# A decoder step on one core: how the kernel picks a free buffer, by the engine that used it last

## The chip, the cores and the metric

The kernel runs on one core of a Trainium2 chip. The metric is the device time of one execution in microseconds (us), the median of several runs. The core has a matrix engine (TensorE, PE in the profile, its weight loads PEld), three engines for element-wise work (VectorE or DVE, ScalarE or ACT, GpSimd or POOL), and SyncE (SP), which only starts transfers here. GpSimd starts transfers too: loads leave from SP's queue, intermediate stores from POOL's.

## The reference

One inference step of a small hybrid decoder, 1024 prompt tokens and 8 single-token samples, 2048 channels, in fp32. Layer 1 projects to a branch and a gate, pools the branch over trailing windows of 2, 4, 8 and 16 tokens, mixes groups of 512 channels, multiplies by silu(gate) and projects back. Layer 2 does sliding-window attention (128 tokens, 32 heads over 4 shared key/value heads, with sinks) on keys and values made from layer 1's output. Each layer ends in a layer norm.

```python
z = x @ w_in                                  # layer 1
u, gate = z[..., :D_POOL], z[..., D_POOL:]
d, new_state = multiscale_pool(u, prefix, pos)
d = jnp.einsum('btgc,gce->btge', d.reshape(...), w_grp).reshape(B, T, D_POOL) * scale
x = layer_norm(ALPHA * x + (d * jax.nn.silu(gate)) @ w_out, g_ln, b_ln)
k, v = shared_kv(x, pos, w_kv)
z = x @ w_in_b                                # layer 2
q, gate = rope_partial(z[..., :D_ATTN], pos), z[..., D_ATTN:]
o = attn_core(q, k, v, q_pos, k_pos, sinks)
x = layer_norm(ALPHA * x + (o * jax.nn.silu(gate)) @ w_out_b, g_ln, b_ln)
```

## The kernel before

**Tiles and phases.** The tokens are split into two chunks of 512 and 520 (512 prompt tokens and the 8 samples). Activations lie with channels on the 128 partitions and tokens along the free dimension. Ten phases run one after another (PHASES): `ai` (input projection, pooling and group mix of layer 1), `ao` (its output projection and norm), `bi` (keys, values, queries, gates and attention of layer 2), `bo` (output projection and norm), each for chunk 0 and chunk 1. Most phases multiply with Strassen's scheme: seven products of half width for a block of two by two (`seven`, L655 to L657), two start with plain products (`unit`, L683 to L685).

**fp32 by two parts.** Each weight tile and each activation tile is split in a high part, cast by ScalarE (L476 for weights, L766 for activations), and a low part, which VectorE subtracts (L491 and L775). Each product is three matmuls: high by high, high by low, low by high. One "unit" of a Strassen phase is 24 matmuls of 128x128 by 256 or 260 columns on one weight tile.

**The pipeline.** `begin` runs ahead of each unit e: it issues weight loads up to unit e+7 (`load_to`, L275), casts up to e+4 and subtractions up to e+3 (`cast_to`, `prep_to`). The loaded tile is read by the cast and by the subtraction and is then free; the two parts are free after the unit's matmuls. Results leave PSUM by ScalarE (L594, L600, L603, L609, L615, L628) and VectorE (L616, L621). Beside them run sums of weights for the scheme, made on the fly and stored for the other chunk (L281, L334, L424 to L430), sums of activations (`t_ops`, L823 to L827), pooling (`pool_tile`, L1031 to L1042, split at L263 and L264), the norms (`ln_gen`, `phase_out`, L1234, L1277 to L1289), and attention (rope L1621 and L1729; scores L1759; maxima L1776 to L1788; exponentials L1795; sums L1803; scaling L1808; transposes L1812, copied out at L1821 and L1822; values L1836; gating L1845, stored at L1848). `t_gen` and `sum_gen` are spread between the units as side work.

**What sets the order.** PE, DVE and ACT run in the order of the source: `in_order` ties each instruction to the one before it on its engine. SP and POOL are ordered by the framework's own scheduler. The framework puts a semaphore wait wherever a buffer or a value needs it, also between two instructions of one engine.

**The buffers.** All of this shares one pool, `Mem`: 53 slots of 128 x 1040 fp32, which can be given out whole (`full`) or by halves (`half`). Slots are given and released in the order of the source, long before the engines get there; a slot that is given again makes its first writer wait until the engines have really finished with it. Before the change, `release` stamps a half with a count of releases, plus 10 if it was the source of a store, and `full` and `half` take the slot with the smallest stamp, whoever asks and whoever used it last.

Of the kernel before, what the change touches and what calls it, by code (L numbers as in the profile page):

```python
# [95 lines left out]
class Slot:  # L96
# [14 lines left out]

    def free(self, stored=False):
        self.mem.release(self, 10 if stored else 0)


class View:
# [11 lines left out]

    def free(self):
        for s in self.slots:  # L130
            self.left[s] -= 1
            if not self.left[s]:
                s.free()


class Mem:


    def __init__(self, pool, n):
        self.pool = pool  # L140
        self.t = [None] * n
        self.f = [[0, 0] for _ in range(n)]
        self.clock = self.n = 0
# [39 lines left out]
class Kern:  # L183
# [88 lines left out]
    def load1(self, s, k, src):  # L272
        def go():
            s[k] = self.mem.full()
            self.nc.sync.dma_start(s[k].a[:, :1024], src)  # L275

        return go
# [124 lines left out]
    def sum_gen(self, name):  # L402
# [6 lines left out]
        held = {}  # L409

        def load(n):
            if n < len(parts) and n not in held:
                q, cs = parts[n]
                s = held[n] = self.mem.full()
# [71 lines left out]
    def prep_to(self, n):  # L486
        self.cast_to(n)
        while self.prepped < min(n, len(self.stream)):
            s = self.stream[self.prepped]
            hi, lo = self.hl[self.prepped], self.mem.full()  # L490
            self.nc.vector.tensor_sub(lo.r[:, :1024], s.src().a[:, :1024], hi.a[:, :1024])  # L491
# [75 lines left out]
    def seven(self, c, z0, z1, after, c11=None, split=False, own=None):  # L567
# [65 lines left out]
        def run(idx):  # L633
# [24 lines left out]
            for s in w:  # L658
                s.free()
            for g in range(2):  # L660
# [8 lines left out]
    def unit(self, done):  # L669
# [3 lines left out]
        for par in range(2):  # L673
            w = self.begin()
            wh, wl = (s.r for s in w)
            for k in range(8):
# [11 lines left out]
                if k == 7:  # L688
                    for a in w:
                        a.free()  # L690
                    if par == 1:
                        self.posts.append(lambda: done(ps))
# [47 lines left out]
    def x_load(self):  # L740
# [3 lines left out]
        TH = T // 2  # L744
        s = self.mem.full()
        if self.xseven:
# [63 lines left out]
    def x_used(self, k):  # L810
        if self.last:
            ss = self.X.pop(k)
            if not (self.shared and not self.strassen and k[0] == 1):
                for s in ss:
                    s.free()

    def t_ops(self, E, O, dst, kp, TH):

        nc = self.nc
        s = self.mem.full()  # L820
        t = s.v(4, TH)
# [8 lines left out]
    def t_gen(self, key):  # L830
# [3 lines left out]
        def load(kp):  # L834
            s[kp] = self.mem.full()
            self.nc.sync.dma_start(s[kp].v(2, T), self.act[key][:, 2 * kp : 2 * kp + 2, :])
# [13 lines left out]
    def j_steps(self, T, a, b, box, *free):  # L850

        def add():
            box["u"] = self.mem.half()
            self.nc.vector.tensor_add(box["u"].a[:, :T], a, b)
            for f in free:
                f.free()
# [12 lines left out]
    def j_sum(self, T, box, out):  # L869
# [3 lines left out]
        for s in [slice(0, T)] if T <= 512 else [slice(0, T // 2), slice(T // 2, T)]:  # L873
# [7 lines left out]
            out(s, ps)  # L881
        hl.free()

# [25 lines left out]
    def ln_gen(self, c, pre, acc, gc, bc, out, td):  # L909
# [9 lines left out]
        def load(p):  # L919
            if p < 8 and p not in pre:  # L920
                pre[p] = self.mem.full()
                nc.sync.dma_start(self.pair_view(pre[p], T), away(p))
# [22 lines left out]
        else:  # L945
            self.j_sum32(T, [a2[:, 0], a2[:, 1]], put)
            acc.free()
        yield
        w = self.mem.full()
        q, v = w.a[:, :T], w.a[:, TMAX : TMAX + T]  # L950
# [61 lines left out]
    def pool_tile(self, c, m, Us, ext, dd):  # L1012
# [11 lines left out]
        if ext is not None:  # L1024
            nc.scalar.copy(ext[:, i, :, 15], U[:, NST + TP : NST + T])
        bufs = [self.mem.full() for _ in range(2 if w > 2 else 1)]
        src, step, n = U, 1, 0
# [36 lines left out]
    def group_half(self, c, g, h, dd, sg):  # L1064
# [24 lines left out]
        for s in w:  # L1089
            s.free()  # L1090
        if h == 1:
            for k in range(4):
                dd[k][2].free()

        def post():
            G = self.mem.full()
            t = self.pair_view(G, T)
# [108 lines left out]
    def phase_out(self, c, res, nxt, last=None):  # L1206
# [8 lines left out]
        def x_in(p):  # L1215
            if p < 8:
                xs[p] = self.mem.full()
                nc.sync.dma_start(self.pair_view(xs[p], T), res[:, 2 * p : 2 * p + 2, :])
# [86 lines left out]
    def phase_end(self, c, xs, x_in, pre, acc, gc, bc, out):  # L1305
# [77 lines left out]
        def back(p):  # L1383
            pre[p] = self.mem.full()
            nc.sync.dma_start(tv(p), self.act["p", c][:, 2 * p : 2 * p + 2, :])
# [222 lines left out]
    def partner(self, s, n, T):  # L1608

        t = self.mem.full()  # L1610
        for a in range(4):
# [131 lines left out]
    def attend(self, c, t, at, s1, s2, late=False, ticks=CLOSE):  # L1743
# [8 lines left out]
        def score():  # L1752
# [10 lines left out]
            if lastq:  # L1763
                s.free()

# [44 lines left out]
        def turn():  # L1810
            for i in range(8):
                nc.tensor.transpose(  # L1812
                    PT[:, i * P : (i + 1) * P], x["sc"][:, i * P : (i + 1) * P], cst[:, K_ID : K_ID + P]
                )
            x["s"].free()

        def keep():


            x["w"], x["wp"] = self.mem.full(), self.mem.full()  # L1820
            nc.scalar.copy(x["w"].a[:, :1024], PT)  # L1821
# [6 lines left out]
        def values():  # L1828
            o = x["o"] = self.S[:, 1, :512] if late else self.psO()
            for b in range(NB):  # L1830
                bs = slice(b * P, (b + 1) * P)
                for n, (V, p) in enumerate(((self.V[b + 1], x["w"].a), (self.Vd[b], x["wp"].a))):
                    for j in range(2):
# [4 lines left out]
                        )  # L1838
            x["w"].free()
            x["wp"].free()  # L1840

        def gate():
            a = self.ao[c, t] = self.mem.half()
            z, j = self.sg.pop((c, t))
# [42 lines left out]
    def dec_keys(self, pr):  # L1887
        nc, io = self.nc, self.io
        s = self.dks = self.mem.full()
        dk = s.a[:, :1024].rearrange("p (b k) -> p b k", b=NDEC)  # L1890
# [8 lines left out]
    def decode(self, c, pr):  # L1899
# [7 lines left out]
        def v0():  # L1907
            x["v"] = self.mem.full()
            dv = x["dv"] = x["v"].a[:, :1024].rearrange("p (b k) -> p b k", b=NDEC)
# [421 lines left out]
```

## Time and profile before

| | |
|---|---|
| median of 3 runs | 2347.38 us (2345.62 to 2347.71) |
| the profiled execution | 2344.57 us |
| its span, first to last instruction | 2342.8 us |
| TensorE busy, share of the span | 98% |
| VectorE, ScalarE, GpSimd busy | 82%, 58%, 9% |
| granted TensorE clock, mean | 0.997 |
| transferred | 669.39 MB, mean 286 GB/s |

The times of the lines below are in us from the start of the span. "L491" is line 491 of the kernel; "m<-m,m" says which buffers are written and read (m is the pool, pD, pO, pS are PSUM, names like swob are DRAM). "[1.02 <-DVE m L491]" is the idle time ahead of an instruction and what ended it. In a list of waits, the three numbers are us in total, how often, and the longest. Some per cent of matmul records may be missing in a trace.

### The profile page before, as it was taken

The numbers are of one execution on the slowest core, as the hardware profiler recorded it, in microseconds if no ns is written. First come the engines' busy times: TensorE is split into PE (matmuls) and PEld (weight loads), VectorE is DVE, ScalarE is ACT, GpSimd is POOL, SyncE is SP. The second block draws the span as 40 slices with busy tenths as digits, with TensorE's granted clock in tenths as the row PEclk, the third lists the DMA queues.
The fourth block names the chain that finished last, engine by engine and source line by source line (L and its number), as shares of the span: only waits on it lengthen the run. The fifth ranks groups of instructions, "written<-read, shape, count | busy, mean of one in ns | idle before, by whom it ended". The sixth has DMA issues, their size and how long they took to land. (4 is left out here: it accounts for less than half of the span.)

```text
span 2342.8 us, 49652 instructions
## 1 busy us (share of the span) xinstructions
PE 2302.7 (98%) x19960; PEld 2202.7 (94%) x19960; DVE 1923.7 (82%) x2386; ACT 1365.4 (58%) x2502; POOL 202.3 (9%) x379
## 2 busy tenths in 40 slices
PE   8999999999999999999999999999999999999997
PEld 6899999999999999998777899999999999999997
DVE  8788988777878878868998898897777778889887
ACT  4454446544546557655464666685666668556656
POOL 0111110010000000000111111100000000000000
PEclk9999999999999999999999999999999999999999
DMA  8668789989889989999799766788776768699785
GB/s 293 213 242 310 272 287 343 328 290 326 299 302 328 323 286 329 320 339 325 262 330 360 254 235 225 253 297 279 249 249 231 231 199 299 230 355 371 268 303 196
DMA packets 252072, 669.39 MB, mean 286 GB/s; under 512 B 25760, under 2 KB 106560, under 8 KB 251840
## 3 DMA queue, kind: packets, MB, share of 16 engines
q1 hardware_dynamic: 206368, 501.14, 63.3%
q0 software_dynamic: 45472, 165.07, 18.2%
q8 instruction: 156, 2.56, 0.4%
q14 instruction: 76, 0.62, 0.1%
HBM read 471.01 MB, written 185.59 MB: 280 GB/s over the span
## 5 line engine op out<-in xcount | busy, mean ns | idle before, releaser
L655 PE MATMUL pD<-m,m 128*128 128x260 f32 (+1 forms) x4752 | 1346.2, 283 | 4.7 <-ACT pD L594 2.8
L657 PE MATMUL pD<-m,m 128*128 128x260 f32 (+1 forms) x4752 | 1340.3, 282 | 6.2 <-DVE m L491 6.1
L656 PE MATMUL pD<-m,m 128*128 128x260 f32 (+1 forms) x4752 | 1339.8, 282 | 1.1 <-DVE m L775 1.1
L491 DVE TENSOR_TENSOR m<-m,m 128x1024 fp32r<-128x1024 f32 x674 | 814.2, 1219 | 114.8 <-ACT m L476 59.7
L655 PEld LDWEIGHTS pD<-m,m 128*128 128x128 f32 x4752 | 895.5, 188 | 13.2 <-issue 5.1
L657 PEld LDWEIGHTS pD<-m,m 128*128 128x128 f32 x4752 | 895.9, 189 | 8.5 <-DVE m L491 8.5
L656 PEld LDWEIGHTS pD<-m,m 128*128 128x128 f32 x4752 | 895.5, 188 | 1.8 <-DVE m L775 1.3
L476 ACT CAST m<-m 128x1024 fp32r<-128x1024 f32 x674 | 703.4, 1049 | 251.5 <-DVE m L334 69.6
L683 PE MATMUL pD<-m,m 128*128 128x512 f32 x448 | 179.5, 401 | 8.1 <-ACT m L766 8.1
L684 PE MATMUL pD<-m,m 128*128 128x512 f32 x448 | 177.2, 395 | 1.0 <-DVE m L775 1.0
L685 PE MATMUL pD<-m,m 128*128 128x512 f32 x448 | 177.0, 395 | 0.0
L775 DVE TENSOR_TENSOR m<-m,m 128x1024 fp32r<-128x1024 f32 (+1 forms) x120 | 146.9, 1225 | 6.9 <-ACT m L766 5.4
L766 ACT CAST m<-m 128x1024 fp32r<-128x1024 f32 (+1 forms) x120 | 125.8, 1052 | 14.1 <-PE pD L684 5.2
L683 PEld LDWEIGHTS pD<-m,m 128*128 128x128 f32 x448 | 84.6, 189 | 29.5 <-ACT m L766 8.1
L334 DVE TENSOR_TENSOR m<-m,m 128x1024 f32<-128x1024 f32 x88 | 107.6, 1222 | 4.3 <-DMA m<-in_wia 2.6
L684 PEld LDWEIGHTS pD<-m,m 128*128 128x128 f32 x448 | 84.6, 189 | 20.8 <-DVE m L775 2.1
L685 PEld LDWEIGHTS pD<-m,m 128*128 128x128 f32 x448 | 84.5, 189 | 19.7
L616 DVE TENSOR_TENSOR m<-pD,m 128x260 f32<-128x260 f32 (+1 forms) x86 | 36.0, 419 | 80.6 <-ACT pD L615 73.8
L628 ACT COPY m<-pD 128x260 f32<-128x260 f32 (+1 forms) x83 | 31.0, 374 | 117.9 <-PE pD L657 117.8
L1795 ACT ACTIVATE m<-m,sm 128x128 f32<-128x128 f32 x256 | 99.2, 391 | 0.0
L1085 PE MATMUL pD<-m,m 128*128 128x260 f32 (+1 forms) x528 | 91.5, 323 | 0.0
L1808 ACT ACTIVATE m<-m,sm 128x128 f32<-128x128 f32 x256 | 81.9, 392 | 12.8 <-DVE sm L1803 12.8
(245 smaller groups left out, 2113.1 us busy)
## 6 DMA issues: line engine op xcount, KB each, us to landing
m<-in_wia SPq DMA_DIRECT2D x124, 512.0 KB
m<-in_wib SPq DMA_DIRECT2D x120, 512.0 KB
swia<-m POOLq DMA_DIRECT2D x64, 512.0 KB, 4.8
m<-swia SPq DMA_DIRECT2D x64, 512.0 KB
m<-swoa SPq DMA_DIRECT2D x64, 512.0 KB
swib<-m POOLq DMA_DIRECT2D x64, 512.0 KB, 5.4
m<-swib SPq DMA_DIRECT2D x64, 512.0 KB
m<-swob SPq DMA_DIRECT2D x56, 512.0 KB
```

The source lines that it names most:

```text
L334: self.nc.vector.tensor_add(s[out].a[:, :1024], s[x].a[:, :1024], s[y].a[:, :1024])
L476: self.nc.scalar.copy(hi.r[:, :1024], self.stream[self.cast].src().a[:, :1024])
L491: self.nc.vector.tensor_sub(lo.r[:, :1024], s.src().a[:, :1024], hi.a[:, :1024])
L655: nc.tensor.matmul(ps[:, :TH], wh[:, s], h, start=new and k == 0, stop=False, skip_group_check=on)
L656: nc.tensor.matmul(ps[:, :TH], wh[:, s], l, start=False, stop=False, skip_group_check=on)
L657: nc.tensor.matmul(ps[:, :TH], wl[:, s], h, start=False, stop=k == 7, skip_group_check=on)
L683: nc.tensor.matmul(ps[:], wh[:, s], h, start=par == 0 and k == 0, stop=False)
L684: nc.tensor.matmul(ps[:], wh[:, s], l, start=False, stop=False)
L685: nc.tensor.matmul(ps[:], wl[:, s], h, start=False, stop=par == 1 and k == 7)
L766: self.nc.scalar.copy(h.r[:, :n], s.a[:, :n])
L775: self.nc.vector.tensor_sub(l.r[:, :n], s.a[:, :n], h.a[:, :n])
L1795: nc.scalar.activation(x["s3"][:, i, :], x["s3"][:, i, :], AF.Exp, bias=nm[:, i : i + 1], scale=0.125, accum_out=rs[:, i : i + 1],)
```

## The change

Each release now carries the engine that used the buffer last: `p` TensorE, `v` VectorE (the default), `s` a store. Each request says who writes first: `v` VectorE, `a` ScalarE and the rest (the default), `d` a transfer. READY holds, for each kind of writer, how much older or younger a release by each engine counts. A transfer sees TensorE's buffers as they are, VectorE's as 4 releases younger, a store's as 10; ScalarE and the rest see VectorE's as 6 and a store's as 14 younger. All take the oldest by that measure, but for VectorE: if any whole buffer was released by VectorE alone, it takes the newest of these. `half` counts ages in the same way and falls back on `oldest("a")`. Some forty call sites name the engine; sizes, counts of slots, the order of the source and all arithmetic stay. The core of the diff:

```diff
+READY = {"v": {"p": 0, "v": 0, "s": 10}, "d": {"p": 0, "v": 4, "s": 10}, "a": {"p": 0, "v": 6, "s": 14}}
...
-    def free(self, stored=False):
-        self.mem.release(self, 10 if stored else 0)
+    def free(self, stored=False, by="v"):
+        self.mem.release(self, "s" if stored else by)
...
-        self.f = [[0, 0] for _ in range(n)]
+        self.f = [[(0, "p"), (0, "p")] for _ in range(n)]
...
-    def full(self):
-        i = min(self.whole(), key=lambda i: max(self.f[i]))
+    def age(self, h, by):
+        return h[0] + READY[by][h[1]]
+
+    def oldest(self, by):
+        w = self.whole()
+        if by == "v":
+            own = [i for i in w if self.f[i][0][1] == self.f[i][1][1] == "v"]
+            if own:
+                return max(own, key=lambda i: max(self.f[i]))
+        return min(w, key=lambda i: max(self.age(h, by) for h in self.f[i]))
+
+    def full(self, by="a"):
+        i = self.oldest(by)
...
-    def half(self):
-        part = [(a if b is None else b, i) for i, (a, b) in enumerate(self.f) if (a is None) != (b is None)]
+    def half(self, by="a"):
+        part = [
+            (self.age(a if b is None else b, by), i)
+            for i, (a, b) in enumerate(self.f) if (a is None) != (b is None)
+        ]
...
-        i = min(part)[1] if part else min(self.whole(), key=lambda i: max(self.f[i]))
+        i = min(part)[1] if part else self.oldest("a")
...
-    def release(self, s, late):
+    def release(self, s, by):
...
-            self.f[s.i][h] = self.clock + late
+            self.f[s.i][h] = self.clock, by
...
-            s[k] = self.mem.full()
+            s[k] = self.mem.full("d")
             self.nc.sync.dma_start(s[k].a[:, :1024], src)
...
-            hi, lo = self.hl[self.prepped], self.mem.full()
+            hi, lo = self.hl[self.prepped], self.mem.full("v")
             self.nc.vector.tensor_sub(lo.r[:, :1024], s.src().a[:, :1024], hi.a[:, :1024])
...
             for s in w:
-                s.free()
+                s.free(by="p")
...
-        l = self.mem.full()
+        l = self.mem.full("v")
         self.nc.vector.tensor_sub(l.r[:, :n], s.a[:, :n], h.a[:, :n])
```

The other sites follow the same pattern: `full("d")` ahead of every load, `full("v")` or `half("v")` where VectorE writes first, `free(by="p")` where matmuls read last.

More of the change, by code (lines that the diff above doesn't have):

```diff
@@ L127, in __getitem__, with free @@
         return self.slots[kp // 2].rv(2, self.t)[:, kp % 2, self.cs]
-    def free(self):
+    def free(self, by="p"):
         for s in self.slots:
@@ L658, in run @@
             for s in w:
-                s.free()
+                s.free(by="p")
             for g in range(2):
@@ L689, in unit @@
                     for a in w:
-                        a.free()
+                        a.free(by="p")
                     if par == 1:
@@ L744, in x_load @@
         TH = T // 2
-        s = self.mem.full()
+        s = self.mem.full("d")
         if self.xseven:
@@ L852, in add @@
         def add():
-            box["u"] = self.mem.half()
+            box["u"] = self.mem.half("v")
             self.nc.vector.tensor_add(box["u"].a[:, :T], a, b)
@@ L881, in j_sum @@
             out(s, ps)
-        hl.free()
+        hl.free(by="p")
     def j_sum32(self, T, src, out):
@@ L1025, in pool_tile @@
             nc.scalar.copy(ext[:, i, :, 15], U[:, NST + TP : NST + T])
-        bufs = [self.mem.full() for _ in range(2 if w > 2 else 1)]
+        bufs = [self.mem.full("v") for _ in range(2 if w > 2 else 1)]
         src, step, n = U, 1, 0
@@ L1763, in score @@
             if lastq:
-                s.free()
+                s.free(by="p")
         def select():
@@ L1838, in values @@
                         )
-            x["w"].free()
-            x["wp"].free()
+            x["w"].free(by="p")
+            x["wp"].free(by="p")
         def gate():
-            a = self.ao[c, t] = self.mem.half()
+            a = self.ao[c, t] = self.mem.half("v")
             z, j = self.sg.pop((c, t))
```

34 lines of the change are left out of this document (17 added, 17 removed).

## The prediction

> **What bounds the kernel now.** The page comes first, then the busy time by stretch (PE, PEld, DVE, ACT and POOL busy us with instruction counts, granted clock, DMA share, GB/s), then the list of waits. The reader is to see how little there is to win.
>
> ```profile
> span 2342.8 us, 49652 instructions
> ```
> ```profile
> PE 2302.7 (98%) x19960; PEld 2202.7 (94%) x19960; DVE 1923.7 (82%) x2386; ACT 1365.4 (58%) x2502; POOL 202.3 (9%) x379
> ```
> ```profile
> 0.00:58.60 58.60, 49.53 (x204) 39.41 (x205) 49.01 (x59) 26.98 (x34) 4.99 (x16) 1.00 0.80 293
> 58.60:2284.00 2225.40, 2207.59 (x19434) 2121.29 (x19433) 1829.13 (x2257) 1301.63 (x2400) 191.66 (x355) 1.00 0.83 288
> 2284.00:2342.80 58.80, 45.56 (x326) 42.01 (x324) 45.54 (x72) 36.76 (x70) 5.68 (x9) 0.92 0.54 196
> ```
>
> TensorE idles 2342.8 - 2302.7 = 40.1 us: 9.1 at the start, 13.2 at the end, 17.8 between. The listing of compiled instructions shows TensorE's order unchanged, and in the first and last 58 us VectorE gets three added waits in all. So a gain comes out of the 17.8 us, 0.76% of the span. Who ends those waits (total, times, longest):
>
> ```profile
> PE pD L657 <- DVE m L491: 6.1, 10, 1.4
> PE pS L1759 <- DVE m L1729: 3.4, 4, 1.5
> PE pD L655 <- ACT pD L594: 2.8, 2, 1.9
> ```
>
> TensorE waits mostly for a late VectorE. VectorE and ScalarE in turn lose time to buffers:
>
> ```profile
> ACT m L476 <- DVE m L491: 44.4, 27, 6.1
> ```
> ```profile
> DVE m L491 <- PE pD L656: 9.9, 8, 2.5
> ```
> ```profile
> SPq L275 <- PE pD L657: 459.2, 176, 8.7
> SPq L275 <- DVE m L491: 187.8, 94, 5.7
> ```
>
> The cast L476 reads a loaded tile and does not need L491's result; its 44.4 us are waits for a buffer that VectorE still reads. L491 in its turn waits for a buffer that TensorE still reads, and SP's queue of weight loads stands 459 us for TensorE's buffers and 188 us for VectorE's, early enough that no load is late for it.
>
> **What the change moves.** I compared both listings, which name every instruction's buffers and waits. VectorE's 2387 rows keep their order but for some 50 of one stretch, ScalarE's but for one, and no compute is added. SP has 994 rows for 989 and POOL 382 for 381, because a listing row can merge several transfers; none is added. The buffers differ. Of the L491 subtractions, 552 write a buffer that VectorE itself touched last (232 before) and 90 one of TensorE's (388 before). Of the L476 casts, 51 take a buffer of VectorE's (209 before) and 600 one of TensorE's (400). And 385 VectorE instructions now wait on the VectorE instruction directly ahead, 13 no longer do: 372 more.
>
> **The price of such a wait.** The same operation and size, two in a row, without and with it (start, us together, what), and one alone (busy, mean ns):
>
> ```profile
> 2174.51 2.36 DVE L491 TENSOR_TENSOR m<-m,m 128x1024 fp32r<-128x1024 f32 x2
> ```
> ```profile
> 2022.10 2.48 DVE L334 TENSOR_TENSOR m<-m,m 128x1024 f32<-128x1024 f32 x2
> ```
> ```profile
> L491 DVE TENSOR_TENSOR m<-m,m 128x1024 fp32r<-128x1024 f32 x674 | 814.2, 1219 | 114.8 <-ACT m L476 59.7 <-issue 13.8 <-PE pD L656 9.9
> L334 DVE TENSOR_TENSOR m<-m,m 128x1024 f32<-128x1024 f32 x88 | 107.6, 1222 | 4.3 <-DMA m<-in_wia 2.6
> ```
>
> One takes 1.22 us either way, two take 2.36 or 2.48. The second L334 overwrites what the first reads and carries the wait; the second L491 does not, and starts 0.08 us before the first has ended. So a wait costs 2.48 - 2.36 = 0.12 us, and 372 come to 45 us of VectorE time. VectorE idles 2225.4 - 1829.1 = 396 us in the middle, which hides most of it. The bounds are 0 and 45 us; what counts is where VectorE has no gap and TensorE is already at its heels. There are two such stretches:
>
> ```profile
> 897.23:944.03 46.80, 46.74 (x392) 46.53 (x391) 46.80 (x45) 37.36 (x48) 1.07 (x2) 1.00 0.92 332
> 2131.53:2175.60 44.07, 42.49 (x353) 41.85 (x351) 44.07 (x41) 35.36 (x47) 1.07 (x2) 1.00 0.99 363
> ```
> ```profile
> PEld pD L657 <- DVE m L491: 0.3, 1, 0.3
> ```
> ```profile
> PE pD L657 <- DVE m L491: 1.0, 2, 0.7
> ```
>
> ```profile
> 933.36 1.22 DVE L491 TENSOR_TENSOR m<-m,m 128x1024 fp32r<-128x1024 f32 x1
> ```
> ```profile
> 2167.65 1.22 DVE L491 TENSOR_TENSOR m<-m,m 128x1024 fp32r<-128x1024 f32 x1
> ```
>
> VectorE is busy 46.80 of 46.80 us and 44.07 of 44.07. In the first stretch TensorE (PEld is its weight load) waits once for L491, the one at 933.4; in the second twice, 0.7 and 0.3 us, the last time for the one at 2167.7. Up to 933.4 the first gains 18 waits and loses 1; up to 2167.7 so does the second. Each costs 17 x 0.12 = 2.0 us, all on TensorE's path, as nothing there absorbs it. Four smaller places where TensorE already waits for VectorE (near 1355, 2021 to 2051, 2114 and 2300) have 10 such waits not covered by slack: 1.2 us. **Loss: 2.0 + 2.0 + 1.2 = 5.2 us.**
>
> **What the freed waits return.** I went through TensorE's stalls, looked for a buffer wait in the chain ahead, and asked of the compiled order whether it goes.
>
> ```profile
> 355.77 1.04 ACT L476 CAST m<-m 128x1024 fp32r<-128x1024 f32 x1 [6.87 <-DVE m L621]
> ```
> ```profile
> 726.23 1.05 ACT L476 CAST m<-m 128x1024 fp32r<-128x1024 f32 x1 [5.64 <-DVE m L491]
> ```
> ```profile
> 1515.85 0.37 ACT L600 COPY m<-pD 128x256 f32<-128x256 f32 x1 [3.24 <-DMA to<-m]
> ...
> 1525.26 1.05 ACT L476 CAST m<-m 128x1024 fp32r<-128x1024 f32 x1 [1.02 <-DVE m L491]
> ```
> ```profile
> 1517.21 1.22 DVE L491 TENSOR_TENSOR m<-m,m 128x1024 fp32r<-128x1024 f32 x1 [2.42 <-ACT m L476]
> ```
> ```profile
> PE pS L1759 <- DVE m L1729: 1.3, 1, 1.3
> PE pD L643 <- ACT m L628: 1.2, 1, 1.2
> ```
> ```profile
> 1813.46 1.05 ACT L476 CAST m<-m 128x1024 fp32r<-128x1024 f32 x1 [3.02 <-DVE m L1729]
> ```
> ```profile
> PE pO L1836 <- DVE m L1822: 0.4, 1, 0.4
> ```
>
> At 355.77 the cast held ScalarE 6.87 us, and the negation L594 queued behind it came late for TensorE: the 1.9 us of the list above. Its new buffer was last used near 339, so the 1.9 goes. At 726.23 the new buffer is again one that L491 has just read, so that stall stays. At 1515.85 ScalarE waited 3.24 us for a store to leave a buffer, then L491 2.42 us for ScalarE, then TensorE 1.3 for L1729. The new buffer is free by 1512, and 1.3 goes. The cast at 1525.26 gets one free since 1518: of L643's 1.2 us, 1.0 goes. At 1813.46 the buffer is free 3.8 us sooner and the 0.4 goes. **Gain: 1.9 + 1.3 + 1.0 + 0.4 = 4.6 us.** What is late next at 359 is L491 itself, which I took as just in time.
>
> Moved and costed at nothing: ScalarE meets 17 buffers that TensorE frees after the instruction would have started, 24 us by the times of this trace, the longest 4.3 us (L962 near 1111). ScalarE's 924 idle us in the middle cover them; uncovered they bound this at 24 us. A wait of that kind, 8.4 us long, stands in the trace beside no TensorE stall:
>
> ```profile
> ACT m L476 <- PE pO L1085: 24.9, 3, 8.4
> ```
>
> Weight loads leave earlier, since VectorE no longer drains the common queue of free buffers: 1.8 us on average by the release times of this trace. Everything queued on SP behind a blocked load moves with it. Between nothing and the waits for loads, of which these are the largest, I take nothing:
>
> ```profile
> ACT m L476 <- DMA m<-swob: 7.4, 6, 2.1
> ```
> ```profile
> ACT m L476 <- DMA m<-in_wia: 6.6, 6, 3.3
> ```
>
> POOL's transfers wait for VectorE's sums, not for free buffers, and its memsets still come before their readers.
>
> **Sum.** +5.2 - 4.6 = +0.6 us: 2344.57 of the profiled execution becomes 2345.2, and the median of the runs shown, 2.8 above it, 2347.38 + 0.6 = 2348.0.
>
> **The rivals.**
>
> *Waits on the own engine are free.* If 2.48 against 2.36 belongs to L334 and not to the wait, only the gain is left: 2347.4 - 4.6 = 2342.8, or somewhat under with earlier loads. For it speaks that the pair with the wait is another line; against it, that both lines have the same operation and size, and one alone takes the same time. The Trainium skill says this of VectorE (VectorE: DVE Perf Modes, The DRAIN you can't avoid): the next operation starts only once the pipeline is empty, so that in a chain "the semaphore costs nothing extra". By that rule the time would be this rival's. The pair of 2.36 us, whose second starts before the first ends, does not agree.
>
> *Earlier loads clear the second stretch.*
>
> ```profile
> 2130.18 1.05 ACT L476 CAST m<-m 128x1024 fp32r<-128x1024 f32 x1 [1.76 <-DMA m<-swob]
> ```
> ```profile
> 2131.53 1.23 DVE L1234 SCALAR_TENSOR_TENSOR m<-m,m 128x1024 f32<-128x1024 f32 x1 [1.85 <-ACT m L628]
> ```
> ```profile
> PE pD L655 <- ACT m L609: 0.5, 1, 0.5
> ```
>
> L628 ran late behind a cast that waited for a load from swob; VectorE, which idled 1.85 us for it, could start its stretch about that much earlier. Then 2.0 of the loss goes, and 1.5 us of stalls inside it (0.7, 0.5, 0.3): 2348.0 - 3.5 = 2344.5. Against it: those two loads get buffers released no earlier than before.
>
> *Slower: the stalls pass to VectorE.* ScalarE is on time near 359, 1522 and 1816, but TensorE then waits for the next subtraction, which the added waits hold back. The price is the loss without the gain: 2347.4 + 5.2 = 2352.6. It decides if VectorE has no gap in the few us ahead of these places. For it stands that VectorE's first gap after 344 is this one of 0.50 us; against it, that at 1517 it had 2.42 us.
>
> ```profile
> 357.37 0.69 DVE L264 TENSOR_TENSOR m<-m,m 128x512 fp32r<-128x512 f32 x1 [0.50 <-ACT m L263]
> ```
>
> *The buffers do not change hands as said.* The compiled order excludes nearly all of this: 2347.4.
>
> **How the numbers follow.** Forecast 0.45, free waits 0.12, earlier loads 0.15, stalls passed on 0.25, nothing moved 0.03. 0.2% of 2347.4 is 4.7 us, about what a measurement of this kernel can tell from no change: faster means below 2342.7, slower above 2352.1. Faster holds the free waits and about half of the earlier loads, where stalls elsewhere shrink too: 0.20. Slower is the passed-on stalls, 0.25. The rest is 0.55. The range reaches a little past both outer rivals, 2341.5 to 2353.5; the forecast's own is 2344 to 2351.
>
> **What would show it.** Right: pairs of L491 at 2.48 us; near 933 and 2168 TensorE waits for L491 about 2 us longer; the stalls near 359 and 1522 are gone; ScalarE's waits for L491 fall from 44.4 us to under 15; TensorE's idle time stays within 3 us of 40. Wrong: L491 pairs still at 2.36 us (free waits), or stalls near 359 and 1522 that now name L491 or L1729 (passed on).

## The result, and the profile after

The changed kernel takes 2355.97 us (median of 6 runs, 2354.18 to 2358.9) against 2347.09 us of the kernel before in the same job: the ratio is 1.004, with a 95% interval of 1.0029 to 1.005. It is slower by 8.9 us, and the forecast of 2348.0 us with its range up to 2353.5 us missed it.

The profiled execution took 2355.04 us, 10.5 us more than that of the kernel before. Line numbers are 15 higher than in the kernel before for nearly all lines that matter here: L491 is now L506, L476 is L491, L655 to L657 are L670 to L672, L275 is L290. The page first:

```profile
span 2353.2 us, 49647 instructions
...
PE 2306.5 (98%) x19960; PEld 2205.6 (94%) x19960; DVE 1949.7 (83%) x2386; ACT 1361.7 (58%) x2502; POOL 202.3 (9%) x379
```

VectorE is busy 26.0 us longer, and not because its instructions are longer: they add up to 2.7 us more, while the time in which one overlaps the next falls from 124.9 to 101.5 us. TensorE idles 2353.2 - 2306.5 = 46.7 us instead of 40.1 us. The middle of the span, cut as in the prediction (PE, PEld, DVE, ACT and POOL busy us, granted clock, DMA share, GB/s), and the waits of TensorE, ScalarE and SP's queue (total us, times, longest):

```profile
58.60:2294.40 2235.80, 2210.61 (x19434) 2123.60 (x19433) 1855.40 (x2260) 1298.22 (x2399) 191.16 (x355) 1.00 0.81 286
```
```profile
PE pD L672 <- DVE m L506: 10.5, 14, 1.7
...
PE pD L670 <- ACT m L643: 2.2, 1, 2.2
PE pD L658 <- ACT m L643: 2.1, 1, 2.1
...
PE pS L1698 <- ACT m L2023: 1.5, 1, 1.5
```
```profile
ACT m L491 <- DVE m L506: 14.4, 5, 6.1
```
```profile
SPq L290 <- PE pD L672: 325.2, 150, 10.5
SPq L290 <- DMA swoa<-m: 97.1, 18, 8.0
SPq L290 <- DVE m L506: 80.7, 45, 8.4
SPq L290 <- DMA swob<-m: 80.2, 14, 8.7
```

In the middle TensorE idles 2235.8 - 2210.6 = 25.2 us where it idled 17.8. It waits for L506 10.5 us (6.1 before), and three stalls of 1.5 to 2.2 us are new. The waits of ScalarE's casts for L491 (now L506) fell from 44.4 to 14.4 us, as the change means them to. Those of SP's weight loads for it fell too (187.8 to 80.7), but SP now stands for stores: 97.1 us for those to swoa, where it stood

```profile
SPq L275 <- DMA swoa<-m: 32.5, 8, 9.6
```

in the kernel before. All waits of SP for stores, added up over the rows of the list, are 659 us, 269 before.

**Where the time went.** TensorE's order is the same in both kernels, so each of its instructions can be matched, and the start after minus the start before is its delay (of one profiled execution each). It runs so (us of the kernel before, growth of the delay): 340 to 365 -1.0; 905 to 950 +3.3; near 1129 +1.7; near 1355 +0.8; 1524 -1.35; 1532 +0.9; 1666 +0.55; 1817 -0.55; 1950 to 1980 +3.3; 2021 to 2051 +0.6; 2100 to 2130 +0.9; 2130 to 2190 +1.5; the rest is under half a microsecond. The larger places are read below.

**Between 905 and 950.** VectorE, before and after (start, us, what):

```profile
929.87 1.22 DVE L491 TENSOR_TENSOR m<-m,m 128x1024 fp32r<-128x1024 f32 x1
931.00 1.24 DVE L775 TENSOR_TENSOR m<-m,m 128x1040 fp32r<-128x1040 f32 x1
...
935.64 1.22 DVE L491 TENSOR_TENSOR m<-m,m 128x1024 fp32r<-128x1024 f32 x1
936.78 1.24 DVE L775 TENSOR_TENSOR m<-m,m 128x1040 fp32r<-128x1040 f32 x1
937.93 1.22 DVE L491 TENSOR_TENSOR m<-m,m 128x1024 fp32r<-128x1024 f32 x1
```
```profile
931.45 1.23 DVE L506 TENSOR_TENSOR m<-m,m 128x1024 fp32r<-128x1024 f32 x1
932.77 1.24 DVE L790 TENSOR_TENSOR m<-m,m 128x1040 fp32r<-128x1040 f32 x1
...
937.96 1.23 DVE L506 TENSOR_TENSOR m<-m,m 128x1024 fp32r<-128x1024 f32 x1
939.27 1.24 DVE L790 TENSOR_TENSOR m<-m,m 128x1040 fp32r<-128x1040 f32 x1
940.61 1.23 DVE L506 TENSOR_TENSOR m<-m,m 128x1024 fp32r<-128x1024 f32 x1
```

The same instructions, each as long as before, start 1.13 to 1.15 us after one another in the first fence and 1.31 to 1.34 us in the second. So a wait on the instruction directly ahead costs 0.18 us here, not the 0.12 us of the forecast. The size was to be had before the change: this pair of L491 in the kernel before waits too, beside the 2.36 us of the pair that does not.

```profile
2115.78 2.54 DVE L491 TENSOR_TENSOR m<-m,m 128x1024 fp32r<-128x1024 f32 x2
```

Over the whole trace after, the gap between two such instructions (L506, L790 or L349 second, gaps above 150 ns left out) has a median of -83 ns without the wait (461 pairs; the second starts before the first ends), of 34 ns with it where the second waits for at most two semaphores in all (102 pairs), and of 91 ns where it waits for three or more (230 pairs). In the kernel before, the wait had three or more in 9 pairs of 55. VectorE lost 3.2 us up to the L491 of 933.4, over 18 waits; TensorE's delay grew by 3.3.

**Near 1129.** TensorE waits 1.5 us for a ScalarE copy (L2023, L2008 before). The chain goes back to VectorE's rope (L1621 before, L1636 after), which waits for a transfer from SP. SP's queue and that wait, before and after:

```profile
1103.86 1.22 SPq L417 DMA_DIRECT2D m<-in_wob  x2
1105.17 2.51 SPq L1613 DMA_DIRECT2D m<-m  x4
```
```profile
1111.60 1.23 DVE L1621 TENSOR_TENSOR m<-m,m 128x1024 f32<-128x1024 f32 x1 [3.48 <-DMA m<-m]
```
```profile
1105.26 3.00 SPq L432 DMA_DIRECT2D m<-in_wob  x4
1108.35 2.52 SPq L1628 DMA_DIRECT2D m<-m  x4
```
```profile
1115.35 1.23 DVE L1636 TENSOR_TENSOR m<-m,m 128x1024 f32<-128x1024 f32 x1 [5.24 <-DMA m<-m]
```

Four weight loads go ahead of the exchange of halves (m<-m) instead of two, after a wait for a store; rope waits 1.8 us longer.

**Near 1532 and 1971.** ScalarE's casts wait for loads, and the copies queued behind them (L643) come late for TensorE:

```profile
1529.44 1.05 ACT L491 CAST m<-m 128x1024 fp32r<-128x1024 f32 x1 [2.20 <-DMA m<-in_wkv]
```
```profile
1969.46 1.05 ACT L491 CAST m<-m 128x1024 fp32r<-128x1024 f32 x1 [3.24 <-DMA m<-in_wob]
```
```profile
1971.00:1976.60 5.60, 3.71 (x31) 3.49 (x30) 5.50 (x8) 5.60 (x12) 0.54 (x1) 1.00 1.06 384
1976.65:1980.05 3.40, 3.13 (x14) 3.13 (x15) 3.22 (x4) 3.37 (x10) 0.00 (x0) 0.50 1.04 398
```

The second stall has a tail: TensorE was busy 3.71 of 5.60 us, and in the next 3.4 us its granted clock is 0.50. Both together make the 3.3 us. The kernel before has such a stretch too, from 1357.4 on, and the kernel after has it there from 1362.3 on, so it does not show in the difference.

### The profile page after: what moved, and what is told of

It is laid out like the page before. It is cut to its first block, busy times and chain, and to the rows that moved or that the text cites. A ratio compares the mean times of both kernels' runs of the same rounds, so it can differ in the third digit from the quotient of the medians.

```text
span 2353.2 us, 49647 instructions
## 1 busy us (share of the span) xinstructions
PE 2306.5 (98%) x19960; PEld 2205.6 (94%) x19960; DVE 1949.7 (83%) x2386; ACT 1361.7 (58%) x2502; POOL 202.3 (9%) x379
## 5 line engine op out<-in xcount | busy, mean ns | idle before, releaser
L670 PE MATMUL pD<-m,m 128*128 128x260 f32 (+1 forms) x4752 | 1349.0, 284 | 7.0 <-ACT pD L609 3.1
L672 PE MATMUL pD<-m,m 128*128 128x260 f32 (+1 forms) x4752 | 1343.2, 283 | 10.5 <-DVE m L506 10.5
L670 PEld LDWEIGHTS pD<-m,m 128*128 128x128 f32 x4752 | 897.1, 189 | 15.7 <-issue 5.3
L672 PEld LDWEIGHTS pD<-m,m 128*128 128x128 f32 x4752 | 897.6, 189 | 13.7 <-DVE m L506 13.6
L506 DVE TENSOR_TENSOR m<-m,m 128x1024 fp32r<-128x1024 f32 x674 | 820.5, 1221 | 97.5 <-ACT m L491 61.7
L491 ACT CAST m<-m 128x1024 fp32r<-128x1024 f32 x674 | 702.3, 1048 | 184.3 <-DVE m L349 80.4
L790 DVE TENSOR_TENSOR m<-m,m 128x1024 fp32r<-128x1024 f32 (+1 forms) x120 | 147.6, 1230 | 13.4 <-ACT m L781 6.4
L349 DVE TENSOR_TENSOR m<-m,m 128x1024 f32<-128x1024 f32 x88 | 107.6, 1223 | 3.6 <-DMA m<-in_wib 1.8
L643 ACT COPY m<-pD 128x260 f32<-128x260 f32 (+1 forms) x83 | 31.0, 373 | 129.0 <-PE pD L672 128.9
L1810 ACT ACTIVATE m<-m,sm 128x128 f32<-128x128 f32 x256 | 99.3, 391 | 0.0
L609 ACT ACTIVATE pD<-pD 128x260 f32<-128x260 f32 (+1 forms) x84 | 31.1, 370 | 110.4 <-PE pD L672 110.1
```

What stands on the lines that cost most here:

```text
L349: self.nc.vector.tensor_add(s[out].a[:, :1024], s[x].a[:, :1024], s[y].a[:, :1024])
L491: self.nc.scalar.copy(hi.r[:, :1024], self.stream[self.cast].src().a[:, :1024])
L670: nc.tensor.matmul(ps[:, :TH], wh[:, s], h, start=new and k == 0, stop=False, skip_group_check=on)
L672: nc.tensor.matmul(ps[:, :TH], wl[:, s], h, start=False, stop=k == 7, skip_group_check=on)
L1810: nc.scalar.activation(x["s3"][:, i, :], x["s3"][:, i, :], AF.Exp, bias=nm[:, i : i + 1], scale=0.125, accum_out=rs[:, i : i + 1],)
```

## The experiments

Theory 1: VectorE's waits on itself are the loss. Theory 2: it is what ScalarE and the transfers now pick. More came as these failed; they are stated in the expectations. Ratios are to the kernel before in the same job, with 95% intervals. "Waits on itself" counts VectorE instructions that wait on the one directly ahead: 655 before, 1028 after, by the compiled listings.

**One half of the change each.**

```diff
-READY = {"v": {"p": 0, "v": 0, "s": 10}, "d": {"p": 0, "v": 4, "s": 10}, "a": {"p": 0, "v": 6, "s": 14}}
+READY = {"v": {"p": 0, "v": 0, "s": 10}, "d": {"p": 0, "v": 0, "s": 10}, "a": {"p": 0, "v": 0, "s": 10}}
```

> VectorE still takes its own newest buffer, but ScalarE and the transfers rank all buffers alike again (only a store counts 10 younger, as in the kernel before). 1011 VectorE instructions wait on the one directly ahead, against 1028 after the change and 655 before it. Theory 1 (the loss of 8.9 us comes from VectorE's waits on itself: 356 more of 0.12 us, of which those where TensorE follows VectorE closely count): 2352 to 2356, and TensorE's delay against the kernel before grows by 2 us or more between 905 and 950 and again between 2100 and 2190. Theory 2 (it comes from what ScalarE and the transfers now pick): near the kernel before, 2345 to 2349, and the new stalls near 1129 and 1971 are gone.

2356.95 us, 1.0048 (1.0035 to 1.0060); the delay grew by 3.3 between 905 and 950 and by 2.5 between 2130 and 2190, by 0.9 near 1129 and not at all near 1971.

```diff
-            if own:
+            if False:
```

> The other half of the change: ScalarE and the transfers rank buffers as in the change, VectorE takes the oldest buffer like everyone. 662 VectorE instructions wait on the one directly ahead, 7 more than before the change. Theory 1 (VectorE's waits on itself): 2344 to 2348, no growth of the delay between 905 and 950. Theory 2 (the other picks): 2352 to 2356, with stalls of 1.5 us or more near 1129 and 1971.

2351.51 us, 1.0026 (1.0015 to 1.0038); no growth between 905 and 950, but 1.7 near 1129, 3.1 near 1355 and 4.1 at 1530 to 1540, at the last two with a granted clock of 0.50 for 6.8 us. Near 1971, where theory 2 had a stall, there is none: those 3.3 us come with neither half alone. Each half costs by itself (10.6 and 5.1 us), the whole change less than their sum. Neither theory is enough.

**Not the newest of its own.**

```diff
-                return max(own, key=lambda i: max(self.f[i]))
+                return sorted(own, key=lambda i: max(self.f[i]))[-min(2, len(own))]
```

> The whole change, but VectorE takes the second newest of its own buffers. 818 VectorE instructions wait on the one directly ahead, 210 fewer than after the change. Theory 1: 2349 to 2353, since somewhat over half of the added waits go, the delay between 905 and 950 falls from 3.3 us to under 1.5. Theory 2: as after the change, 2354 to 2357, as ScalarE and the transfers meet much the same buffers.

2353.46 us, 1.0036 (1.0024 to 1.0048).

```diff
-                return max(own, key=lambda i: max(self.f[i]))
+                return min(own, key=lambda i: max(self.f[i]))
```

> The whole change, but VectorE takes the oldest of its own buffers. 802 VectorE instructions wait on the one directly ahead. Theory 1: 2349 to 2353, like the second newest. Theory 2: as after the change, 2354 to 2357.

2351.55 us, 1.0022 (1.0013 to 1.0031). Both have no growth between 905 and 950 (0.2 and 0.05 us), as theory 1 says, but a new stall of 6.2 and 5.3 us at 2115, where VectorE waits for a store or a load that is late. So the waits of the first stretch are a cost that can be switched off, and something else comes in its place.

**Are loads that wait for stores the rest?**

```diff
-READY = {"v": {"p": 0, "v": 0, "s": 10}, "d": {"p": 0, "v": 4, "s": 10}, "a": {"p": 0, "v": 6, "s": 14}}
+READY = {"v": {"p": 0, "v": 0, "s": 10}, "d": {"p": 0, "v": 4, "s": 24}, "a": {"p": 0, "v": 6, "s": 28}}
```

> The whole change, but for transfers a buffer of a store counts 24 releases younger (10 in the change) and for ScalarE 28 (14). Theory 2, narrowed (loads at the head of SP's queue wait for stores that still read their buffers, and all transfers behind them are late): SP's waits for stores fall from some 540 us to under 300, the stalls near 1129 and 1971 go, and the time falls by 3 to 5 us to 2351 to 2353; the delay between 905 and 950 stays at 3.3 us. If the loads do not matter, the time stays at 2355 to 2357. VectorE's waits on itself are as before this edit (1019 against 1028).

2368.19 us, 1.0090 (1.0074 to 1.0105): 12 us slower than the change itself. SP's waits in this kernel, and ScalarE's for one of the weights:

```profile
SPq L290 <- PE pD L672: 518.3, 201, 9.5
```
```profile
ACT m L491 <- DMA m<-in_wib: 19.8, 8, 7.7
```

The waits for stores did fall (659 to 296 us in all), and the stalls that the narrowed theory 2 names shrank: 1.7 to 0.0 us near 1129, where the exchange now waits for its source alone (1.3 us) and not behind loads, and 3.3 to 1.1 near 1971. Whether the stores had made them stays open, since SP still stands 7.0 and 5.4 us for a store ahead of the two places. And SP now stands 518 us for TensorE's buffers, and other loads are late: the delay grows by 9.0 us between 2100 and 2130, where VectorE waits 7.1 us for a load of "o". The time is against the theory. That fewer buffers are left to choose from while the stored ones are kept back is the likely reason, and not shown.

```diff
-READY = {"v": {"p": 0, "v": 0, "s": 10}, "d": {"p": 0, "v": 4, "s": 10}, "a": {"p": 0, "v": 6, "s": 14}}
+READY = {"v": {"p": 0, "v": 0, "s": 24}, "d": {"p": 0, "v": 4, "s": 24}, "a": {"p": 0, "v": 6, "s": 28}}
...
-            if own:
+            if False:
```

> VectorE takes the oldest buffer like everyone, and a store's buffer counts 24 to 28 releases younger instead of 10 to 14: neither VectorE's waits on itself (676) nor loads held by stores. If theories 1 and 2 together explain the loss, the gains of the change near 361, 1524 and 1817 (3 us together) are left over: 2343 to 2346. If it stays at 2350 or above, a third cause is at work.

2361.74 us, 1.0065 (1.0052 to 1.0077). By the expectation a third cause is at work. This kernel too keeps stored buffers back, now from VectorE as well, and 7.1 us of its delay come between 2100 and 2130, as in the kernel above and in the next one.

```diff
-        self.mem.release(self, 10 if stored else 0)
+        self.mem.release(self, 24 if stored else 0)
```

> The kernel before with one number changed: a stored buffer counts 24 releases younger instead of 10. A control: another shuffle of the buffers without the change. If the time depends on the two named costs alone, it stays within 3 us of the kernel before (2343 to 2349); if the order of the kernel before is simply a lucky one that any shuffle spoils, it is 2350 or above.

2362.77 us, 1.0061 (1.0049 to 1.0074), with 7.9 us of it between 2100 and 2130, where VectorE waits 6.0 us for a load of "o". Without the change, one other age of the stored buffers costs more than the change does.

```diff
-READY = {"v": {"p": 0, "v": 0, "s": 10}, "d": {"p": 0, "v": 4, "s": 10}, "a": {"p": 0, "v": 6, "s": 14}}
+READY = {"v": {"p": 0, "v": 0, "s": 10}, "d": {"p": 0, "v": 4, "s": 10}, "a": {"p": 0, "v": 6, "s": 14}, "n": {"p": 8, "v": 0, "s": 14}}
...
-            sq, sqs = self.mem.full(), {}
+            sq, sqs = self.mem.full("n"), {}
...
-                    sqs[p - 1] = sq if p == 1 else self.mem.full()
+                    sqs[p - 1] = sq if p == 1 else self.mem.full("n")
```

> The whole change, but the squares of the second norm prefer VectorE's buffers (TensorE's count 8 younger), so they wait for no matmul. If the stall near 1129 comes from those squares holding ScalarE, it goes (1.7 us); if it comes from the partner transfer that SP issues late behind loads waiting for a store, it stays at 1.5 us or more.

One run, 2363.72 us. The stall near 1129 stayed (2.2 us), as it would if it comes from the exchange on SP's queue. The whole was 8 us slower than the change for a handful of other buffers, which no theory had said: the delay grew by 3.1 us near 1666 and by 4.9 between 2100 and 2130 (0.55 and 0.9 in the changed kernel).

**The idea without the shuffle.** Everyone ranks as before. VectorE takes one of its own buffers, and the oldest gets that one's place in the list (`real` keeps who really used a buffer last; the full edit also sets READY back to the ranks of the kernel before):

```diff
...
+        i = min(w, key=lambda i: max(self.age(h, by) for h in self.f[i]))
+        own = [j for j in w if self.real[j][0][1] == self.real[j][1][1] == "v"]
+        own.sort(key=lambda j: max(self.real[j]))
+        if by == "v" and own:
+            j = own[-1]
+            self.f[i], self.f[j] = self.f[j], self.f[i]
+            return j
+        return i
...
```

> Everyone ranks buffers as in the kernel before; VectorE's writes take its own newest buffer, and the buffer that it would have taken (the oldest) goes back to the list with that one's place, so the pattern of the list stays that of the kernel before. 1008 VectorE instructions wait on the one directly ahead (655 before). Theory 1 (VectorE's waits on itself): the delay grows by 3.3 us between 905 and 950 and by 2.5 to 3 between 2130 and 2190, and the time is 2350 to 2354. Theory 3 (a tuned order of buffers and transfers, which any shuffle spoils): the same plus late loads, 2355 or above. If the waits cost nothing: 2345 to 2348.

2355.81 us, 1.0041 (1.0027 to 1.0054). And against that kernel, the second newest:

```diff
-        if by == "v" and own:
-            j = own[-1]
+        if by == "v" and len(own) > 1:
+            j = own[-2]
```

> The same exchange with VectorE's second newest buffer: 675 VectorE instructions wait on the one directly ahead, 20 more than before the change. No growth of the delay between 905 and 950 by any theory. Theory 1 alone: 2343 to 2348. Theory 3 (any shuffle spoils): 2349 or above, with late loads at the same places as in the other variants (near 1355, 1971 or 2115).

2350.08 us, 1.0018 (1.0009 to 1.0027). The two differ in 333 waits on itself, and by 5.7 us in the median. TensorE's waits between 905 and 955, of the first and of the second kernel (the second has none there):

```profile
PE pD L676 <- DVE m L510: 1.9, 2, 1.2
PE pD L674 <- ACT pD L613: 0.6, 1, 0.6
```

Between 2131 and 2200, the newest and the second newest:

```profile
PE pD L676 <- DVE m L510: 3.2, 3, 1.3
PE pD L674 <- ACT pD L634: 1.2, 1, 1.2
```
```profile
PE pD L674 <- ACT pD L634: 2.2, 1, 2.2
PE pD L676 <- DVE m L510: 0.7, 2, 0.4
```

The delay grew by 3.2 and 2.7 us in the two stretches with the newest buffer, by 0.4 and -1.0 us with the second newest. In the first stretch this is theory 1 by itself, and the same holds for all kernels without a pinned order: of the six that take the newest (the change among them) each grew by 3.2 to 3.3 us between 905 and 950, of the nine others none by more than 0.4. In the second stretch the six grew by 1.2 to 3.5 us and the nine others by -2.0 to 0.4. There the difference is not the wait alone: the kernel with the second newest stalls for 4.6 us between 2100 and 2130, ahead of the stretch (1.8 with the newest), and VectorE can catch up meanwhile.

**A shuffle without intention.**

```diff
-        self.mem.release(self, 10 if stored else 0)
+        self.mem.release(self, 11 if stored else 0)
```

> The kernel before with a stored buffer counted 11 releases younger instead of 10: the smallest shuffle, with no intention. VectorE's waits on itself stay at 655. Theory 3: 2349 or above, stalls at the places of the other variants. Otherwise, if the change's own choices are what costs, within 2 us of the kernel before: 2344 to 2349.

2351.33 us, 1.0018 (1.0009 to 1.0027), about 4 us by the ratio, which leaves out one execution of 3758.52 us. With 9 instead of 11:

> The kernel before with a stored buffer counted 9 releases younger instead of 10: a second shuffle without intention, 238 of 1126 transfers change place on SP. If the order of the kernel before is a tuned one that any shuffle spoils: 2349 to 2353. If age 11 was bad luck: 2345 to 2348.

2348.05 us, 1.0008 (0.9999 to 1.0017): 1.8 us, not told from nothing. In both a cast waits for in_wkv near 1530 and TensorE behind it. In the kernel with 11 (the profiled execution is its fastest, 2347.32 us):

```profile
ACT m L476 <- DMA m<-in_wkv: 4.1, 2, 3.8
```
```profile
PE pD L643 <- ACT m L628: 3.2, 1, 3.2
```

So a small shuffle without intention cost 4 us once, of stalls at the places of the other variants (1532 and 2115 here), and nothing that this measures the other time. That any shuffle spoils the order, as theory 3 has it, is not shown.

**The queue and its order.** First the exchange and the loads of t_gen on POOL's queue:

```diff
-            self.nc.sync.dma_start(s[kp].v(2, T), self.act[key][:, 2 * kp : 2 * kp + 2, :])
+            self.nc.gpsimd.dma_start(s[kp].v(2, T), self.act[key][:, 2 * kp : 2 * kp + 2, :])
...
-            self.nc.sync.dma_start(t.a[32 * a : 32 * a + 32, : n * T], s.a[32 * b : 32 * b + 32, : n * T])
+            self.nc.gpsimd.dma_start(t.a[32 * a : 32 * a + 32, : n * T], s.a[32 * b : 32 * b + 32, : n * T])
```

> The whole change, but the exchange of halves for rope (partner) and the loads of the side sums (t_gen) leave from POOL's queue instead of SP's, where they stand behind weight loads that wait for buffers. Theory 2 (transfers late on SP's queue): the stalls near 1129 and 2115 go, 2351 to 2354. If the queue does not matter: 2355 to 2357; if POOL's stores hold them longer: above 2357, with the stall near 1129 larger.

2363.97 us, 1.0073 (1.0060 to 1.0086): near 1129 the stall grew from 1.7 to 3.2 us, and 4.2 us came at 440. The exchange near 1129 is not held at the issue here: it leaves as soon as ScalarE has written what it reads. But rope starts 7.9 us after the last of its four issues, 4.5 us in the changed kernel. So the run does not tell what the place in SP's queue is worth. Then SP's compiled order was pinned to that of the other kernel (SP_STEP is a list of 1126 numbers: how far from its place in the source the transfer stands that comes k-th in that order):

```diff
...
+    sp = [i for i in tc.nc.cur_bb.bb.instructions if i.engine == mybir.EngineType.SP and "DMA" in type(i).__name__]
+    for k in range(1, len(sp)):
+        a, b = (sp[j + SP_STEP[j]] for j in (k - 1, k))
+        tc.add_manual_dep(
+            b, a.name, mybir.DependencyInfo(mybir.DependencyClass.NoSync, mybir.DependencyReason.DATA),
+            reason="order of another kernel",
+        )
...
```

> The changed kernel with SP's transfers issued in the order of the kernel before. Theory 4 (the rest of the loss is SP's order: a load that is put ahead waits for its buffer and holds the transfers behind it): 2350 to 2353, the stalls near 1129 and 1971 go, the growth between 905 and 950 stays at 3.3 us. If the buffers themselves are to blame: 2355 to 2357.

2377.54 us, 1.0131 (1.0117 to 1.0145). Near 1129 the exchange is not held behind loads (it waits 0.2 us for its source) and the stall is gone, and 1.0 us is left near 1971, much as theory 4 has it; but new stalls elsewhere cost far more.

> The kernel before, with the same buffers, but SP's transfers in the order of the changed kernel. Theory 4: 2349 to 2353, with stalls near 1129, 1971 or 2115. If the order does not matter: 2345 to 2348.

2439.24 us, 1.0384 (1.0369 to 1.0399).

> VectorE's second newest buffer by exchange (675 waits on itself, 655 before), SP in the order of the kernel before. Theory 4: 2343 to 2347, neither of the two costs is left. If the buffers themselves are to blame: 2349 to 2351 as without the pinned order.

2387.39 us, 1.0177 (1.0159 to 1.0195).

> VectorE's newest buffer by exchange (1008 waits on itself), SP in the order of the kernel before. Theory 4: only the waits on itself are left, 2350 to 2353, 5 to 7 us over the same kernel with the second newest buffer, 3.3 us of it between 905 and 950. If the buffers themselves are to blame: 2355 to 2357.

2363.03 us, 1.0064 (1.0052 to 1.0077). By its times theory 4 fell: 16 to 92 us slower than the kernel before, all four. An order that was compiled for other buffers fits badly. In the kernel before under the order of the changed one SP's weight loads stand 291.9 us for the subtraction (187.8 before), and ScalarE's casts for one of the weights (4.2 us before):

```profile
ACT m L487 <- DMA m<-in_wib: 47.4, 13, 18.3
```

It shows how much late loads can cost, not that the order spoiled the change.

**The gains alone.** Four requests of ScalarE take TensorE's oldest buffer by exchange; 20 of 1126 transfers change place (the other ranks are those of the kernel before):

```diff
...
+CASTS, OUTS = (101, 437, 520), (51,)
...
+        if by == "c":
+            j = min(w, key=lambda i: max(self.age(h, by) for h in self.real[i]))
+            self.f[i], self.f[j] = self.f[j], self.f[i]
+            return j
...
-            hi = self.mem.full()
+            hi = self.mem.full("c" if self.cast in CASTS else "a")
...
-            o["s"] = self.mem.half()
+            o["s"] = self.mem.half("c" if self.n_o in OUTS else "a")
...
```

> The kernel before, but at four requests only (the casts at 355.8, 1525.3 and 1813.5, and the copy at 1515.9 us) ScalarE takes TensorE's oldest buffer by exchange, so that the list keeps its pattern; 20 of 1126 transfers change place on SP. The prediction's gain alone: 4.6 us, 2342 to 2343. By the trace of the changed kernel, where 1.2, 1.35 and 0.5 us went at 362, 1524 and 1817: 3 us, 2343 to 2345. If such a gain is always taken back downstream: 2346 to 2348.

2345.01 us, 0.9993 (0.9984 to 1.0002): no difference that this measures, 1.2 us by the medians. TensorE's waits between 350 and 365, before and in this kernel, and between 1515 and 1545 in this one:

```profile
PE pD L655 <- ACT pD L594: 1.9, 1, 1.9
PE pD L657 <- DVE m L491: 1.2, 1, 1.2
```
```profile
PE pD L676 <- DVE m L509: 2.4, 1, 2.4
PE pD L674 <- ACT pD L612: 0.6, 1, 0.6
```
```profile
PE pD L662 <- ACT m L647: 3.9, 1, 3.9
```

At 359 the wait only changed its name: 3.1 us before, 3.0 us now, on VectorE. At 1524 the 1.36 us came, as they did in the kernels with the ages 9, 11 and 24, which did not aim at them. At 1532, where the next casts wait for in_wkv, 2.7 us went, and 1.4 more right behind it, where the granted clock is 0.50 from 1534.9 on for 3.4 us. Such a stretch of the kernel before, from 1357.4 on, is missing here, and 1.5 us came back there. At 1816 nothing came. No kernel that was tried beats the one before by more than the measurement can tell.

## Why the prediction was wrong

**The price of a wait** (2.48 - 2.36 = 0.12 us) is the first step that failed, by its size. It was read from a pair of L334, the second of which waits for that one semaphore alone; most of the added waits stand on L491 and L775, which wait for loads and casts too, and there it is 0.17 to 0.18 us (91 + 83 ns; 3.2 us over 18 waits). The rows of the kernel before had the L491 pair of 2.54 us. Counted as in the prediction (17, 17 and 10 waits), the loss of 5.2 us becomes 44 x 0.18 = 7.9 us.

**The first stretch** (2.0 us) had the right place and cause and nearly the right count (18 waits, not 17), and cost 3.3 us; shown by the kernels with and without the newest buffer.

**The second stretch** (2.0 us) cost VectorE 3.2 us between its start and the L491 of 2167.7, as the price says, but TensorE only 1.5 us: VectorE entered it 1.7 us less late than TensorE (delays 7.1 and 8.8 us). That is the mechanism of the rival "earlier loads clear the second stretch", in part. That 2.0 came so near to 1.5 is luck, a price too low against a head start that the sum left out.

**The four small places** (1.2 us) cost 2.3 us, most of it for another reason. The 0.8 us near 1355 is no wait of VectorE on itself: it stands in the kernels with the oldest and second newest buffer too. Of the 0.9 near 2115 VectorE waits 0.6 us for a load of "o". The 0.6 between 2021 and 2051 is what the prediction meant.

**The gain** (4.6 us) is the second step that failed; 2.0 us came. At 362 1.0 of 1.9 us, at 1524 1.35 of 1.3, at 1817 0.55 of 0.4; but at 1532, where 1.0 us was to go, 0.9 us was added, since the casts there run into loads. "L491 itself, which I took as just in time" is what fails at 359 when little else moves: the gain is nothing there by the last experiment. The rival "the stalls pass to VectorE" was right for that place there.

**"I take nothing" for the moved loads** is the third failed step, and the largest: 1.7 us near 1129 and 3.3 near 1971, besides 1532. The forecast took the loads as 1.8 us earlier on average, and SP's queue as "early enough that no load is late for it"; what counts is the one that is late. That the one near 1129 comes from the exchange being held behind loads, two further kernels show: where it was not held (stored buffers kept back, and the changed kernel in the other order) the stall is gone. For the one near 1971 the trace alone speaks, a cast that waits 3.24 us for a load. The forecast also costed ScalarE's added waits for TensorE at nothing, and at the one place that was tried this held: the stall near 1129 looked like them, but stayed when the squares took other buffers.

With these sizes the profiled runs add up: 3.3 + 1.5 + 2.3 for the loss, -2.0 for the gain, 1.7 + 3.3 for late loads, 0.55 near 1666, 10.65 us in all, where the two executions differ by 10.5.

**Of the rivals**, "waits on the own engine are free" is refuted by the gaps of -83 against 34 and 91 ns; the quoted sentence of the Trainium skill (VectorE: DVE Perf Modes, The DRAIN you can't avoid), measured there on a chain of copies, does not hold for these instructions. The result lies above the time of the rival "slower" (2352.6 us), but by other ways than it said: dearer waits and late loads, not stalls passed to VectorE.

**What stays open.** By place 3.3 + 1.5 + 0.6 = 5.4 us are VectorE's waits on itself, and the exchange pair differs by 5.7 us. That is not what leaving the newest buffer alone would win: the whole change with the second newest takes 1.0036 of the time before, against 1.004 with the newest, since a stall at 2115 takes most of it back. For what is left the runs show its kind, late transfers at a few tight places (near 1129, 1355, 1532, 1666, 1971 and 2115), and that one of two small shuffles without intention costs 4 us. They do not show what property of the order before keeps these places on time: neither the waits for stores nor SP's order alone does.

## What to carry to other kernels

A tuned allocation is a schedule: a change of the rule that picks buffers moves later picks and the order of the transfers too, so run a shuffle without intention beside it before you credit or blame the rule. Reuse of a buffer that the same engine has just read is not free where the engine has no gap (3.3 us in one stretch here); the second newest spared that, but did not beat the kernel before. Take the price of a wait from the very line that will carry it, with the semaphores that it waits for already.

## What was not expected of the hardware

A VectorE instruction that waits on the one directly ahead starts 34 ns after its end instead of 83 ns before it, and 91 ns after it if it waits for three or more semaphores in all; without such a wait, three semaphores cost nothing (139 pairs, median -83 ns). And TensorE's granted clock fell to 0.50 for 3.4 us right after 5.6 us in which it had been busy only 3.71 us; where a kernel has one such stretch more or less, the delay moves by 1.4 to 1.5 us (at 1535 and 1360 in the last experiment).
